# A mixture-of-experts trunk: the expert batches' gathers and adding scatters go from 96 rows to 128, with an expert's slots dealt out to other rows

## The chip, the cores and the metric

The kernel runs on one core of one Trainium2 chip. The metric is device time in microseconds (us), the median of several executions of the program. Engines are named as in the profile: PE does matmuls (PEld loads their weights), DVE and ACT do elementwise work, POOL issues indirect transfers and small set-up, SP issues plain transfers. All transfers run on the core's sixteen DMA engines.

## The reference, cut to what matters

One layer: a gated-linear-attention mixer, then a mixture of experts over 2048 tokens of 1024 numbers. Each token picks one of 8 groups and, in it, 2 of 8 experts; there are 64 experts.

```
xs = x_pad[slot_tok].reshape(n_blocks, MOE_BLOCK, dm)      # gather each expert's tokens
hid = jax.nn.silu(xb @ w1[e]) * (xb @ w3[e])               # per expert, FF = 256
return hid @ w2[e]
ys = ys * slot_gate[:, None].astype(ys.dtype)
out = jnp.zeros((n_tok + 1, dm), ys.dtype).at[slot_tok].add(ys)[:n_tok]
```

2048 tokens with 2 experts each over 64 experts make 64 tokens for an expert on average.

## The kernel before

The program has three stages in a row. `phase_gla` is the mixer. `phase_out` does the output projection, the router and the placing of tokens. `phase_moe` runs the 64 experts one after the other, and `phase_tail` normalizes and stores. All products are done in three parts (`mm3`, lines 72 to 74): each operand is split into a rounded part and a remainder.

**Slots.** Every expert has 96 early slots (`CAP`). Slot `c` of expert `e` stands in a table in memory as a pair, token number and gate weight. `first` gives an expert the slot number at which its tokens begin: 0, 4, 8 or 12, by its group. The router fills the table with small indirect scatters (`put`, line 1000). The last three token blocks don't go through the table: `part` compares each token's slot number with the tile `slot` (line 1016), `merge` turns that into a matmul that drops token and weight into the right row, and `merged` adds what the table held (tile `early`, read by six transfers at line 1080). The result is `tok` and `gate`, 96 rows by 64 experts. An empty slot holds a token number past the end, so that an indirect transfer passes over it.

Which row holds which slot is set by `slot` and by the six transfers, in the same way: row 6a+b holds slot 16b+a. Of six rows that follow each other, four hold slots below 64.

**An expert.** SP loads its weights as three tiles of 128 rows by 2048 numbers (1 MB each, line 1146). ACT and DVE split each (lines 1151 and 1154). `gather` (line 1185) fetches the expert's token rows, 4 KB each, from `s_h` in memory into 96 rows of the tile `xb`; there are three such tiles. `xtrans` turns them, `up` and `down_mm` multiply, `down` scales by the gate into the tile `y` (line 1236), and `scatter` (line 1239) adds the rows of `y` onto the rows of `s_X` in memory, as a transfer that accumulates. Gathers and scatters are issued by POOL, in program order; the loads are issued by SP as far ahead as tiles are free.

Of the kernel before, what the change touches and what calls it, by code (L numbers as in the profile page):

```python
# [11 lines left out]
F32 = mybir.dt.float32  # L12
F32R = mybir.dt.float32r
BF16 = mybir.dt.bfloat16
I32 = mybir.dt.int32
U32 = mybir.dt.uint32
AF = mybir.ActivationFunctionType
OP = mybir.AluOpType
# [3 lines left out]
S = 2048  # L22
D = 1024
# [12 lines left out]
E = 64  # L36
FF = 256
GR = 8
# [7 lines left out]
XBS = 3  # L46
YS = 3
MERGE = 3
CAP = 96
ROWS = CAP // 16  # L50
MORE = 128
SLOTS = CAP + MORE * ((S + 12 - CAP + MORE - 1) // MORE)
NSENT = 4 * S
ORDER = [i % GR * (E // GR) + i // GR for i in range(E)]
# [4 lines left out]
def split(nc, hi, lo, src, scale=None, eng=None):  # L59

    eng = eng or nc.vector
    if scale is None:
        nc.scalar.activation(hi, src, AF.Copy)  # L63
        eng.tensor_tensor(lo, src, hi.bitcast(F32), op=OP.subtract)  # L64
    else:
        nc.scalar.activation(hi, src, AF.Copy, scale=scale)
        eng.scalar_tensor_tensor(lo, src, scale, hi.bitcast(F32), op0=OP.mult, op1=OP.subtract)
# [774 lines left out]
def phase_out(tc, c, a, s, slots, ep, ex, one):  # L842

    nc = tc.nc
    with ExitStack() as ctx:
# [9 lines left out]
        iota = one.tile([128, 128], F32, name="iota")  # L855
        nc.gpsimd.iota(iota, pattern=[[1, 128]], base=0, channel_multiplier=0, allow_small_or_imprecise_dtypes=True)

        slot = one.tile([128, CAP], F32, name="slot")
        nc.gpsimd.iota(slot.rearrange("p (a b) -> p a b", b=ROWS), pattern=[[1, 16], [16, ROWS]], base=0, channel_multiplier=0,
                       allow_small_or_imprecise_dtypes=True)  # L860
        diff = one.tile([128, 128], F32, name="rdiff")
        nc.gpsimd.iota(diff, pattern=[[1, 128]], base=0, channel_multiplier=-1, allow_small_or_imprecise_dtypes=True)
        before = one.tile([128, 128], BF16, name="before")
# [4 lines left out]
        nc.gpsimd.memset(seen, 0.0)  # L868

        first = one.tile([1, E], F32, name="first")  # L870
        nc.gpsimd.iota(first.rearrange("p (a b c) -> p a b c", a=GR // 4, b=4), pattern=[[0, GR // 4], [4, 4], [0, E // GR]], base=0,
                       channel_multiplier=0, allow_small_or_imprecise_dtypes=True)
        nc.gpsimd.tensor_copy(seen[0:1, :], first)
        ent = one.tile([128, NT, 2, 2], I32, name="ent")
# [6 lines left out]
        def out_proj(t, k0, k1):  # L881
            if k0 == 0:
                PM[t] = [ps.tile([128, 512], F32, name=f"pm{i}", bufs=2) for i in range(2)]
            ep.mm(PM[t], t, k0, k1)

        def add(t):
            if t in PM:
                ep.add(PM[t], t)
# [120 lines left out]
        def part(t, pos):  # L1009

            oh = R[t][1]
            both = slots.tile(F32)
            rhs = both[:, 0:4 * E].rearrange("p (i w e) -> p i w e", i=2, w=2)
            at = both[:, 4 * E:4 * E + 2 * CAP].rearrange("p (i c) -> p i c", i=2)
            for i in range(2):
                nc.vector.tensor_scalar(at[:, i, :], slot, pos[:, i:i + 1], None, op0=OP.is_equal)
                for w, v in enumerate((gone[:, t - NT + MERGE:t - NT + MERGE + 1], ent[:, t, i, 1:2].bitcast(F32))):
                    nc.scalar.activation(rhs[:, i, w, :], oh[:, i, :], AF.Copy, scale=v)
            MG[t] = both, at, rhs

        def merge(p, ts):

            for t in ts:
                both, at, rhs = MG[t]
                for i in range(2):
                    nc.tensor.matmul(p[0:CAP], at[:, i, :], rhs[:, i].rearrange("p w e -> p (w e)"),
                                     start=(t == NT - MERGE and i == 0), stop=(t == NT - 1 and i == 1))
                slots.free(both)

        def merged(p, early):  # L1030
            nc.vector.tensor_tensor(s["tok"], p[0:CAP, 0:E], early[:, :, 0], op=OP.add)
            nc.vector.tensor_tensor(s["gate"], p[0:CAP, E:], early[:, :, 1].bitcast(F32), op=OP.add)

        s["tok"] = one.tile([CAP, E], I32, name="tok")
        s["gate"] = one.tile([CAP, E], F32, name="gate")
        gone = one.tile([128, MERGE], F32, name="gone")
        nc.gpsimd.iota(gone, pattern=[[128, MERGE]], base=S - 128 * MERGE - NSENT, channel_multiplier=1, allow_small_or_imprecise_dtypes=True)
        for t in (2, 3):
            ep.load_o(t)
            ep.load_x(t)  # L1040
        L = NT - 1
        early = one.tile([CAP, E, 2], I32, name="early")
        nc.vector.tensor_tensor(wr, wr, gcol[:, :, None].to_broadcast([128, NK, GR + E]), op=OP.mult)
        for t in range(2):
            finish(t)
# [27 lines left out]
        out_proj(L, 4, 6)  # L1073
        pos = rank(L - 2)
        part(L - 2, pos)
        logits(L - 1)
        choose(L - 1)
        out_proj(L, 6, NK)
        for b in range(ROWS):
            nc.sync.dma_start(early[b:CAP:ROWS], s["table"].rearrange("(p e) w -> p e w", e=E)[16 * b:16 * (b + 1)])  # L1080
        add(L)
        weigh(L - 1)
        address(L - 2, pos)
# [4 lines left out]
        nc.vector.tensor_tensor(hs, ep.x1[L], gff, op=OP.mult)  # L1088
        slots.free(gff, X[L][0])
        part(L - 1, pos)  # L1090
        logits(L)
        nc.scalar.activation(hs, hs, AF.Copy, scale=X[L][1])
# [6 lines left out]
        weigh(L)  # L1099
        pos = rank(L)  # L1100
        merge(last, range(NT - MERGE, L))
        part(L, pos)
        merge(last, (L,))
        merged(last, early)
        address(L, pos)
        pc = ps.tile([128, 2 * E], F32, name="pl")[:, 0:E]
# [58 lines left out]
def phase_moe(tc, c, a, s, ex, plan, rest):  # L1165
    nc = tc.nc
    with ExitStack() as ctx:
# [3 lines left out]
        xp = ctx.enter_context(tc.tile_pool(name="m_x", bufs=1, side="left", reuse_waits="tile"))  # L1171
        ex.add(left, WIDE[1])
        ident = c["ident"]
        tok = s["tok"]
        xbs = [xp.tile([128, D], F32, name=f"xb{i}") for i in range(XBS)]
        spacer = wk.tile([1, 2], F32, name="spacer2", bufs=1)
        scat = []
        XT, HID, UP, HT, PD, Y = {}, {}, {}, {}, {}, {}

        def gather(e):  # L1180
            if e >= E:
                return
            if e < XBS:
                nc.gpsimd.memset(xbs[e][0:CAP, :], 0.0)
            nc.gpsimd.indirect_dma_start(
                out=xbs[e % XBS][0:CAP, :], out_offset=None, in_=s["h"],
                in_offset=bass.IndirectOffsetOnAxis(ap=tok[:, ORDER[e]:ORDER[e] + 1], axis=0),
                bounds_check=S - 1, oob_is_err=False)

        def xtrans(e):  # L1190
            if e >= E:
                return
            p = ps.tile([128, NK, 128], F32, name="ptr")
            x = xbs[e % XBS]
            for k in range(NK):
                nc.tensor.transpose(p[:, k, 0:CAP], x[0:CAP, k * 128:(k + 1) * 128], ident[0:CAP, 0:CAP])
            hi, lo = (xp.tile([128, NK, CAP], F32R, name=n, bufs=2) for n in ("xhi", "xlo"))
            split(nc, hi, lo, p[:, :, 0:CAP])
            XT[e] = hi, lo
# [32 lines left out]
                        (whi[:, ws], wlo[:, ws]), k == 0, k == 1)  # L1232

        def down(e):
            Y[e] = xp.tile([128, D], F32, name="y", bufs=YS)
            nc.scalar.activation(Y[e][0:CAP, :], PD[e][0:CAP, :], AF.Copy, scale=s["gate"][:, ORDER[e]:ORDER[e] + 1])

        def scatter(e):
            st = nc.gpsimd.indirect_dma_start(  # L1239
                out=s["X"], out_offset=bass.IndirectOffsetOnAxis(ap=tok[:, ORDER[e]:ORDER[e] + 1], axis=0),  # L1240
                in_=Y[e][0:CAP, :], in_offset=None, bounds_check=S - 1, oob_is_err=False, compute_op=OP.add)
            for i, o in enumerate(scat):
                if i % GR != e % GR:
                    tc.declare_no_dep(st.ins, o.ins, reason="experts of different groups share no token")
            scat.append(st)
# [8 lines left out]
        for e in range(2):  # L1254
            gather(e)
        ex.split(0, 0, after_gathers)
        for _ in range(WARM):
            nc.tensor.matmul(warm[:, 0:128], ident, ident, start=True, stop=True)
        ex.split(0, 1)
        gather(2)  # L1260
        rest()
        xtrans(0)
        gather(XBS)
        for e in range(E + 1):
            live = e < E
# [23 lines left out]
            if e == 2:  # L1289
                s["plan"] = plan_more(tc, s, plan)  # L1290
        down(E - 1)
        scatter(E - 1)


# [143 lines left out]
def trunk(ctx, tc, a):  # L1438
# [18 lines left out]
    with ExitStack() as main:  # L1457
        big = main.enter_context(tc.tile_pool(name="bigs", bufs=NBIG, side="left"))
        slots = Slots()
        slots.add(big, NBIG)  # L1460
        ep = OutProj(tc, a, s, slots)
        phase_gla(tc, c, a, s, big, ep)
        plan = ctx.enter_context(tc.tile_pool(name="plan", bufs=1, side="right", reuse_waits="tile"))
        one = ctx.enter_context(tc.tile_pool(name="r_one", bufs=1, side="right", reuse_waits="tile"))
        right = ctx.enter_context(tc.tile_pool(name="wide_r", bufs=WIDE[0], side="right", reuse_waits="tile"))
        ex = Experts(tc, a)
        ex.add(right, WIDE[0])
        rest = phase_out(tc, c, a, s, slots, ep, ex, one)
    phase_moe(tc, c, a, s, ex, plan, rest)
    with ExitStack() as main:  # L1470
        big = main.enter_context(tc.tile_pool(name="tails", bufs=NTAIL, side="left", reuse_waits="tile"))
# [47 lines left out]
```

## Time and profile before

| | |
|---|---|
| time, median of 3 runs | 1634.5 us (1633.52 to 1638.4) |
| the profiled execution's own time | 1636.37 us |
| its span, first to last instruction | 1634.6 us |
| PE busy | 1524.8 us (93%) |
| DVE, ACT, POOL busy | 1099.5, 955.0, 338.6 us |
| moved by DMA | 415.22 MB, mean 254 GB/s |

Busy time is time in which an engine has an instruction in work; a matmul's end is modelled, so that a busy PE can still be waiting a little. The granted clock of PE is 0.975 of full speed over the run. The experts run from about 960 us to 1585 us. A view of the transfers gives, for a stretch, each queue's packets, the megabytes, and the time that its packets took as a share of sixteen engines; q1 is the queue of SP's loads and stores, q0 that of POOL's indirect transfers.

### The profile page before, as it was taken

To read this page: it belongs to the slowest core of one execution; us is meant where nothing else is said; L and a number is where in the kernel's file an instruction comes from. 1 tells how busy PE (TensorE), PEld (TensorE's weight loads), DVE (VectorE), ACT (ScalarE), POOL (GpSimd) and SP (SyncE) were. 2 spreads that over 40 slices of the span, in tenths; PEclk is the share of its full clock that TensorE was granted. 3 is DMA by queue.
4 is the path that set the end of the run, shared out by engine and by line. 5 is a ranking of instruction groups with operands and counts; after the bars stand their busy time and mean duration, and the time that the engine had idled before them with its cause. 6 is when DMAs were issued, how large, how long until landed. Compare 5 with 4: busy or idle time off the path is not lost.

```text
span 1634.6 us, 21425 instructions
## 1 busy us (share of the span) xinstructions
PE 1524.8 (93%) x7619; PEld 1194.5 (73%) x7619; DVE 1099.5 (67%) x2087; ACT 955.0 (58%) x1498; POOL 338.6 (21%) x248
## 2 busy tenths in 40 slices
PE   9999999999999999989999879999999999999970
PEld 7877888888888888868888757777766666666640
DVE  6566765566556655553655659989888888888855
ACT  6665544454445544432222358888788777777764
POOL 3211000000000000220211144443343333334320
PEclk9999999999999999989999989999999999999995
DMA  8545834443344434255677388999999999999969
GB/s 306 214 156 214 325 129 156 155 179 131 129 155 164 146 130 155 104 176 192 213 270 269 139 280 308 362 365 361 362 375 368 372 368 365 365 367 371 368 203 396
DMA packets 109117, 415.22 MB, mean 254 GB/s; under 512 B 19489, under 2 KB 35970, under 8 KB 84434
## 3 DMA queue, kind: packets, MB, share of 16 engines
q1 hardware_dynamic: 90242, 379.72, 62.0%
q0 software_dynamic: 15648, 33.83, 8.7%
q8 instruction: 60, 0.98, 0.2%
q10 hardware_dynamic: 3120, 0.30, 0.2%
q14 instruction: 47, 0.39, 0.1%
HBM read 345.53 MB, written 85.02 MB: 263 GB/s over the span
## 4 chain that ended last, share of the span: by engine, by line
PE 60%; DMA 29%; DVE 6%; ACT 2%; issue 1%; SPq 0%; POOL 0%; DVEq 0%; POOLq 0%; ACTq 0%
DMA wide<-w_moe 26%; PE pm L829 9%; PE pvr L72 7%; PE pvr L73 7%; PE pvr L74 7%; PE pu L73 2%; PE pu L74 2%; PE pu L72 2%; PE pk L72 2%; PE pq L72 2%; PE pq L73 2%; PE pq L74 2%; PE pk L73 2%; PE pk L74 2%; PE pl L923 2%
## 5 line engine op out<-in xcount | busy, mean ns | idle before, releaser
L1154 DVE TENSOR_TENSOR wide<-wide 128x2048 fp32r<-128x2048 f32 x192 | 438.2, 2290 | 90.6 <-ACT wide L1151 83.8
L1151 ACT ACTIVATE wide<-wide 128x2048 fp32r<-128x2048 f32 x192 | 366.0, 1914 | 87.3 <-DMA wide<-w_moe 79.2
L1239 POOL DMA_INDIRECT s_X<-y,tok x64 | 162.4, 2538 | 357.3 <-ACT ht L63 251.0
L73 PE MATMUL pu<-wide,xhi 128*96 128x512 f32 x512 | 205.5, 401 | 26.2 <-DVE wide L1154 26.2
L72 PE MATMUL pu<-wide,xhi 128*96 128x512 f32 x512 | 206.9, 404 | 0.9 <-ACT xhi L63 0.9
L74 PE MATMUL pu<-wide,xlo 128*96 128x512 f32 x512 | 203.4, 397 | 0.0
L72 PE MATMUL pvr<-big 128*128 128x512 f32 x504 | 201.3, 399 | 0.0
L73 PE MATMUL pvr<-big 128*128 128x512 f32 x504 | 197.1, 391 | 0.0
L74 PE MATMUL pvr<-big 128*128 128x512 f32 x504 | 196.8, 391 | 0.0
L829 PE MATMUL pm<-big 128*128 128x512 f32 x672 | 162.8, 398 | 5.8 <-DVE big L906 5.8
L829 PEld LDWEIGHTS pm<-big 128*128 128x128 f32 x672 | 125.6, 191 | 31.6 <-DVE big L906 6.2
L64 POOL TENSOR_TENSOR big<-big 128x1024 fp32r<-128x1024 f32 x16 | 39.3, 2468 | 519.3 <-ACT big L63 458.2
L73 PEld LDWEIGHTS pu<-wide,xhi 128*96 128x96 f32 x512 | 83.6, 163 | 71.8 <-DVE wide L1154 42.0
L72 PEld LDWEIGHTS pvr<-big 128*128 128x128 f32 x504 | 94.6, 188 | 20.5
L74 PEld LDWEIGHTS pvr<-big 128*128 128x128 f32 x504 | 94.6, 188 | 20.4
L74 PEld LDWEIGHTS pu<-wide,xlo 128*96 128x96 f32 x512 | 83.4, 163 | 34.0 <-issue 0.8
L73 PEld LDWEIGHTS pvr<-big 128*128 128x128 f32 x504 | 94.7, 188 | 18.0
L72 PEld LDWEIGHTS pu<-wide,xhi 128*96 128x96 f32 x512 | 83.3, 163 | 32.9 <-ACT xhi L63 1.2
L63 ACT ACTIVATE sp<-st 128x256 fp32r<-128x256 f32 x64 | 26.7, 416 | 137.9 <-DVE st L452 125.8
L73 PE MATMUL pd<-wide,ht 128*96 128x512 f32 x256 | 100.9, 394 | 2.2 <-DVE wide L1154 2.2
L72 PE MATMUL pd<-wide,ht 128*96 128x512 f32 x256 | 100.5, 393 | 1.2 <-ACT ht L63 1.2
L74 PE MATMUL pd<-wide,ht 128*96 128x512 f32 x256 | 100.8, 394 | 0.0
(294 smaller groups left out, 2859.5 us busy)
## 6 DMA issues: line engine op xcount, KB each, us to landing
wide<-w_moe SPq DMA_DIRECT2D x192, 1024.0 KB
big<-s_hT SPq DMA_DIRECT2D x96, 512.0 KB
s_hT<-big SPq DMA_DIRECT2D x32, 512.0 KB
s_oT<-big SPq DMA_DIRECT2D x32, 512.0 KB
big<-s_oT SPq DMA_DIRECT2D x32, 512.0 KB
big<-x SPq DMA_DIRECT2D x20, 512.0 KB
big<-w_vr SPq DMA_DIRECT2D x16, 512.0 KB
s_X<-big SPq DMA_DIRECT2D x16, 512.0 KB
```

The source lines that it names most:

```text
L63: nc.scalar.activation(hi, src, AF.Copy)
L64: eng.tensor_tensor(lo, src, hi.bitcast(F32), op=OP.subtract)
L72: nc.tensor.matmul(out, x[0], w[0], start=start, stop=False)
L73: nc.tensor.matmul(out, x[0], w[1], start=False, stop=False)
L74: nc.tensor.matmul(out, x[1], w[0], start=False, stop=stop)
L829: self.nc.tensor.matmul(pm[i], xo[:, sl], w[:, i * 512:(i + 1) * 512], start=(k == 0 and w is whi and xo is hi), stop=(k == NK - 1 and xo ...
L923: nc.tensor.matmul(pl, HT[t][:, k * 128:(k + 1) * 128], wr[:, k, :], start=(k == 0), stop=(k == NK - 1))
L1151: self.nc.scalar.activation(hi, r, AF.Copy)
L1154: self.nc.vector.tensor_tensor(lo, r, hi.bitcast(F32), op=OP.subtract)
L1239: st = nc.gpsimd.indirect_dma_start(out=s["X"], out_offset=bass.IndirectOffsetOnAxis(ap=tok[:, ORDER[e]:ORDER[e] + 1], axis=0), in_=Y[e][0 ...
```

## The change

The gathers and scatters take all 128 rows of `xb`, `tok` and `y`. Slots are dealt out by a table, `DEAL`: its entry (row, at) puts slots at to at+7 into the eight rows row, row+4, ..., row+28. Slots 0 to 63 so come to rows 0 to 31 and 64 to 95, slots 64 to 95 to rows 32 to 63, and rows 96 to 127 stay empty: `slot` holds -1 there, `early` a token number past the end. The products still use rows 0 to 95. An expert's first slot is now its group's number, 0 to 7. The table `early` is read by twelve transfers of eight rows, not six of sixteen. The three `y` tiles are allocated once, and their rows 96 to 127 are set to zero.

```
-ROWS = CAP // 16
+DEAL = [(w, (0, 16, 32, 56)[w]) for w in range(4)] + [(64 + w, (8, 24, 40, 48)[w]) for w in range(4)]
+DEAL += [(32 + w, 64 + 8 * w) for w in range(4)]
...
-        slot = one.tile([128, CAP], F32, name="slot")
-        nc.gpsimd.iota(slot.rearrange("p (a b) -> p a b", b=ROWS), pattern=[[1, 16], [16, ROWS]], base=0, channel_multiplier=0,
-                       allow_small_or_imprecise_dtypes=True)
+        slot = one.tile([128, 128], F32, name="slot")
+        nc.gpsimd.memset(slot[:, CAP:], -1.0)
+        for row, at in DEAL:
+            nc.gpsimd.iota(slot[:, row:row + 32:4], pattern=[[1, 8]], base=at, channel_multiplier=0, allow_small_or_imprecise_dtypes=True)
...
-        nc.gpsimd.iota(first.rearrange("p (a b c) -> p a b c", a=GR // 4, b=4), pattern=[[0, GR // 4], [4, 4], [0, E // GR]], base=0,
+        nc.gpsimd.iota(first.rearrange("p (a b) -> p a b", a=GR), pattern=[[1, GR], [0, E // GR]], base=0,
...
-                nc.tensor.matmul(p[0:CAP], at[:, i, :], rhs[:, i].rearrange("p w e -> p (w e)"),
+                nc.tensor.matmul(p, at[:, i, :], rhs[:, i].rearrange("p w e -> p (w e)"),
...
-        s["tok"] = one.tile([CAP, E], I32, name="tok")
-        s["gate"] = one.tile([CAP, E], F32, name="gate")
+        s["tok"] = one.tile([128, E], I32, name="tok")
+        s["gate"] = one.tile([128, E], F32, name="gate")
...
-        early = one.tile([CAP, E, 2], I32, name="early")
+        early = one.tile([128, E, 2], I32, name="early")
+        nc.gpsimd.memset(early[CAP:, :, 0], NSENT)
+        nc.gpsimd.memset(early[CAP:, :, 1], 0)
...
-        for b in range(ROWS):
-            nc.sync.dma_start(early[b:CAP:ROWS], s["table"].rearrange("(p e) w -> p e w", e=E)[16 * b:16 * (b + 1)])
+        for row, at in DEAL:
+            nc.sync.dma_start(early[row:row + 32:4], s["table"].rearrange("(p e) w -> p e w", e=E)[at:at + 8])
...
+        ys = [xp.tile([128, D], F32, name=f"y{i}") for i in range(YS)]
...
-                out=xbs[e % XBS][0:CAP, :], out_offset=None, in_=s["h"],
+                out=xbs[e % XBS], out_offset=None, in_=s["h"],
...
-            Y[e] = xp.tile([128, D], F32, name="y", bufs=YS)
-            nc.scalar.activation(Y[e][0:CAP, :], PD[e][0:CAP, :], AF.Copy, scale=s["gate"][:, ORDER[e]:ORDER[e] + 1])
+            Y[e] = ys[e % YS]
+            nc.scalar.activation(Y[e][0:CAP, :], PD[e][0:CAP, :], AF.Copy, scale=s["gate"][0:CAP, ORDER[e]:ORDER[e] + 1])
...
-                in_=Y[e][0:CAP, :], in_offset=None, bounds_check=S - 1, oob_is_err=False, compute_op=OP.add)
+                in_=Y[e], in_offset=None, bounds_check=S - 1, oob_is_err=False, compute_op=OP.add)
...
         rest()
+        for y in ys:
+            nc.gpsimd.memset(y[CAP:, :], 0.0)
```

In the program's order the change shows on two engines. On POOL, where the router's tables are set up (`slot`, `rdiff`, `ent`, `gone` are set-up tiles, `s_table` is the table), there stood before:

```order
L856 IOTA iota 128x128
L859 IOTA slot 128x96
L862 IOTA rdiff 128x128
L864 TENSOR_SCALAR before<-rdiff 128x128
L866 MEMSET onesb 128x128
L868 MEMSET seen 128x64
L871 IOTA first 1x64
L873 CAST seen<-first 1x64
L875 IOTA ent 128x32
L1037 IOTA gone 128x3
L999 MEMSET spacer 1x1
L1000 DMA s_table<-ent,addr 137216x2
```

and now:

```order
L862 MEMSET slot 128x32
L864 IOTA slot 128x8 x12
L866 IOTA rdiff 128x128
L868 TENSOR_SCALAR before<-rdiff 128x128
L870 MEMSET onesb 128x128
L872 MEMSET seen 128x64
L875 IOTA first 1x64
L877 CAST seen<-first 1x64
L879 IOTA ent 128x32
L1041 IOTA gone 128x3
L1047 MEMSET early 32x64
L1048 MEMSET early 32x64
```

One set-up instruction became thirteen, and two more stand ahead of the router's first scatter. Further on in POOL's order, where the last scatters into the table (`rest`) are followed by the gathers of experts 3 to 5 and the first adding scatter, there stood:

```order
L999 MEMSET spacer 1x1
L1000 DMA s_table<-ent,addr_9275 137216x2
L1185 DMA xb_9296<-s_h,tok 96x1024
L1185 DMA xb_9297<-s_h,tok 96x1024
L1185 DMA xb_9298<-s_h,tok 96x1024
L1239 DMA s_X<-y,tok 2048x1024
```

and now:

```order
L1004 DMA s_table<-ent,addr_9295 137216x2
L1270 MEMSET y_9319 32x1024
L1270 MEMSET y_9320 32x1024
L1270 MEMSET y_9321 32x1024
L1192 DMA xb_9316<-s_h,tok 128x1024
L1192 DMA xb_9317<-s_h,tok 128x1024
L1192 DMA xb_9318<-s_h,tok 128x1024
L1246 DMA s_X<-y_9319,tok 2048x1024
```

Three memsets come ahead of the gather of expert 3, and each gather writes 128 rows. On SP, at the end of the router, before the experts' loads:

```order
L907 DMA s_h<-big 128x1024
L1080 DMA early<-s_table 16x128 x6
L1095 DMA s_h<-big 128x1024
L897 DMA s_X<-big 128x1024
L1146 DMA wide<-w_moe 128x2048 x13
```

and now:

```order
L911 DMA s_h<-big 128x1024
L1086 DMA early<-s_table 8x128 x12
L1101 DMA s_h<-big 128x1024
L901 DMA s_X<-big 128x1024
L1152 DMA wide<-w_moe 128x2048 x13
```

Six more transfers stand ahead of the last store of `s_h`. PE, DVE and ACT keep their orders; only the shapes of the merge at the end of the router grow from 96 to 128.

## Rows read from the trace of the kernel before

**Rows 1.** Windows in the experts' stage: busy us (instructions) by engine, clock, DMA share, GB/s.

```profile
1050.00:1150.00 100.00, 100.00 (x504) 72.31 (x503) 90.02 (x66) 87.19 (x77) 43.85 (x22) 1.00 1.02 363
1150.00:1550.00 400.00, 374.80 (x1841) 261.50 (x1840) 330.68 (x240) 315.17 (x279) 149.76 (x79) 1.00 1.02 368
```

**Rows 2.** Chain that ended last, two stretches: start us, us, what.

```profile
978.79 0.66 PE ptr L1196 x8
987.94 0.66 PE ptr L1196 x8
...
1043.52 0.66 PE ptr L1196 x8
...
1049.95 25.51 DMA wide<-w_moe
...
1300.79 27.35 DMA wide<-w_moe
```

**Rows 3.** What SP's queue waited for, 1050 to 1550 us: total, times, longest.

```profile
SPq L1146 <- DMA wide<-w_moe: 412.5, 142, 4.8
SPq L1146 <- DVE wide L1154: 9.8, 7, 3.9
```

**Rows 4.** Instructions on tile `y`, 1050 to 1550 us: ACT, then POOL.

```profile
1050.00:1550.00 500.00, 55.87 (x51) 125.96 (x51) 1.00 1.02 367
```

**Rows 5.** DMA queues, 1150 to 1550 us: packets, MB, share of 16 engines.

```profile
q1 hardware_dynamic: 17289, 125.90, 80.7%
q0 software_dynamic: 8960, 20.94, 21.4%
```

**Rows 6.** DMA, 1205.6 to 1209.2 us, between a gather and a scatter.

```profile
DMA packets 251, 1.53 MB, mean 426 GB/s; under 512 B 65, under 2 KB 65, under 8 KB 65
...
q1 hardware_dynamic: 207, 1.52, 101.6%
```

**Rows 7.** DMA, 1200.1 to 1202.6 us, while a scatter runs.

```profile
q0 software_dynamic: 74, 0.27, 53.4%
q1 hardware_dynamic: 68, 0.52, 51.0%
```

**Rows 8.** DMA, 1203.9 to 1205.2 us, while a gather runs.

```profile
DMA packets 72, 0.44 MB, mean 340 GB/s; under 512 B 2, under 2 KB 2, under 8 KB 34
...
q1 hardware_dynamic: 40, 0.31, 79.0%
q0 software_dynamic: 32, 0.13, 32.5%
```

**Rows 9.** DMA, 1264.4 to 1266.6 us, while another gather runs.

```profile
DMA packets 145, 0.68 MB, mean 311 GB/s; under 512 B 42, under 2 KB 42, under 8 KB 81
...
q1 hardware_dynamic: 74, 0.52, 77.2%
```

**Rows 10.** POOL in order of time: start us, us, what, idle before.

```profile
710.93 0.44 POOL L859 IOTA slot<- 128x96 f32 x1
...
713.14 0.13 POOL L1037 IOTA gone<- 128x3 f32 x1
...
760.26 1.13 POOL L1000 DMA_INDIRECT s_table<-ent,addr  x1 [46.92 <-DVE big L839]
...
943.13 0.97 POOL L1184 MEMSET xb<- 96x1024 f32 x1
...
957.53 0.96 POOL L1000 DMA_INDIRECT s_table<-ent,addr  x1 [0.21 <-issue]
958.79 0.98 POOL L1185 DMA_INDIRECT xb<-s_h,tok  x1 [0.31 <-DMA xb<-s_h,tok]
```

**Rows 11.** SP in order of time, the end of the router.

```profile
923.88 3.79 SPq L1080 DMA_DIRECT2D early<-s_table  x6
935.70 0.34 SPq L1095 DMA_DIRECT2D s_h<-big  x1
```

**Rows 12.** Chain that ended last, the experts' first gather and last scatter.

```profile
942.12 9.71 DMA xb<-s_h,tok
...
1580.33 1.65 POOL s_X L1239
```

More of the change, by code (lines that the diff above doesn't have):

```diff
@@ L1013, in part @@
             rhs = both[:, 0:4 * E].rearrange("p (i w e) -> p i w e", i=2, w=2)
-            at = both[:, 4 * E:4 * E + 2 * CAP].rearrange("p (i c) -> p i c", i=2)
+            at = both[:, 4 * E:4 * E + 2 * 128].rearrange("p (i c) -> p i c", i=2)
             for i in range(2):
@@ L1030, in merged @@
         def merged(p, early):
-            nc.vector.tensor_tensor(s["tok"], p[0:CAP, 0:E], early[:, :, 0], op=OP.add)
-            nc.vector.tensor_tensor(s["gate"], p[0:CAP, E:], early[:, :, 1].bitcast(F32), op=OP.add)
-        s["tok"] = one.tile([CAP, E], I32, name="tok")
-        s["gate"] = one.tile([CAP, E], F32, name="gate")
+            nc.vector.tensor_tensor(s["tok"], p[:, 0:E], early[:, :, 0], op=OP.add)
+            nc.vector.tensor_tensor(s["gate"], p[:, E:], early[:, :, 1].bitcast(F32), op=OP.add)
+        s["tok"] = one.tile([128, E], I32, name="tok")
+        s["gate"] = one.tile([128, E], F32, name="gate")
         gone = one.tile([128, MERGE], F32, name="gone")
```

## The prediction

> **What bounds the kernel now.** The change touches the experts' stage, so I look only at where that stage's time goes. The windows come first: from 1050 to 1550 us the sixteen DMA engines have a share of 1.02, that is, no idle time (it passes 1 because neighbouring packets overlap a little), while PE falls from fully busy in the first 100 us to 374.80 of the next 400 [rows 1]. Then the chain of waits: up to 1050 us it runs through PE, whose steps can be read off the transposes of `xb`, one set an expert: 9.15 us from 978.79 to 987.94, and 64.73 us for the seven steps to 1043.52, 9.25 each. From 1049.95 on it runs through the loads, in pieces such as 25.51 and 27.35 us [rows 2]. SP's own waits agree: 412.5 us of that half millisecond until an earlier load had landed, 9.8 for a tile that DVE still read [rows 3]. So PE works off a store of loaded weights at first; later each expert takes what the DMA engines need for it. That is the number to work on.
>
> Its size: an expert's loads are 3.146 MB, so the 125.90 MB that q1 moved in 400 us are 40.0 experts, 10.0 us each [rows 5]. Over 1050 to 1550 us ACT wrote 51 tiles `y` [rows 4]; that is PE's count, which still has its quick first steps in it.
>
> **Where a DMA engine's 10.0 us go.** An expert gives each engine 24 load packets of 8 KB (3.146 MB over 16 engines), and on average 4 gather packets and 4 scatter packets of 4 KB (64 tokens over 16). q1's 80.7% of 400 us over 40 experts is 8.07 us, or 336 ns a packet; q0's 21.4% is 2.14 us [rows 5]. Three short stretches price them.
> - Loads alone: 1.52 MB are 186 packets, 101.6% of 16 engines over 3.6 us is 58.5 us, so 315 ns a packet, at 426 GB/s [rows 6].
> - Beside a scatter: 0.52 MB are 63 packets in 20.4 us, 323 ns; the scatter's 66 take 324 ns each [rows 7]. The two alternate on every engine, and the loads hardly suffer.
> - Beside a gather: 40 packets in 16.4 us, 411 ns, and 32 gather packets in 6.8 us, 211 ns, at 340 GB/s [rows 8]. A second gather: 0.52 MB are 63 packets, 77.2% of 16 engines over 2.2 us is 27.2 us, 430 ns, at 311 GB/s [rows 9].
>
> So a gather slows itself and the loads beside it by a third, a scatter doesn't. A gather writes rows of SBUF, as the loads do; a scatter reads them. The loads write 128 rows and don't slow each other; the gather writes 96. What a gather costs above its bytes is therefore the disputed sum: 24 x (336 - 315) = 0.50 us on the loads, and on the gathers themselves, with 4 x 324 = 1.30 us of the 2.14 for scatters, 0.84 left for four gathers, 0.21 each against half a load packet, 0.157: another 0.21. Together 0.71 of the 10.21 busy us, 7%.
>
> **The change part by part.**
> *Gathers and scatters over 128 rows.* The tokens moved are the same, and the empty rows are passed over now as before (20.94 MB of q0 in 40 experts are 128 packets each, no more than the tokens need [rows 5]). The price of the clash is bounded by 0 (nothing about the gather's packets changes but the rows) and by the whole 0.71 (the gather then behaves like the other transfer that writes 128 rows, the load [rows 6]). I take 0.6: the nearest row is the load's, a little off because overlapped packets are counted twice in a share of 1.02 [rows 1]. That makes 10.0 into 9.4 us.
> The trace shows no rows of a tile, so it can't say which engine writes which. [...]
>
> *How many experts it is worth.* The loads set the pace from 1050 to about 1550 us, 50 experts of 10.0 us: 50 x 0.6 = 30 us. PE has a floor under it: 51 steps [rows 4] of 9.2 us (between 9.15 and 9.25 [rows 2]) are 469 of the 500 us, so no more than 31 can be won. Both limits lie close together, and two streams of nearly one pace wait for each other now and then; I take 27.
>
> [...]
>
> *POOL.* A scatter into the table handles 128 indices in 0.96 us, a gather 96 in 0.98 [rows 10], so 32 more cost between 0 and a third (0.33 us). POOL is busy 149.76 of 400 us [rows 1]: hidden, but for the first gather, on the chain with 9.71 us, and the last scatter, with 1.65 [rows 12]: 0 to 0.3 and 0 to 0.55 us. The set-up's one instruction of 0.44 us becomes thirteen at 0.13 to 0.44, and two memsets: 1.5 to 6 us, ahead of a scatter that sat 46.92 us idle [rows 10]. The three memsets of `y` (at 0.97, like that of `xb`) move the gather of expert 3 from 958.79 by 2.9 us [rows 10]; its rows are wanted at the fourth set of transposes, after 987.94 [rows 2]. Without that cover it would be 2.9 us once.
>
> *SP.* Six reads of `early` took 3.79 us of issue, 0.63 each; twelve take 7.6 and end at 931.5, ahead of the store at 935.70, which waits for its data [rows 11]. Half of them could run into a wait for an earlier one to land, and there are four microseconds for it. Without that cover: at most 3.8 us once, since the first loads queue behind.
>
> *DVE and PE.* Compares and merge over 128 columns in place of 96: the only one on the chain is the last pair, under 0.2 us.
>
> Sum: -27, +0.5 for first gather, last scatter and compares: about -27. The profiled execution took 1636.37 us, 1.8 around its span and 1.9 above the median of the runs; it becomes 1609.4, and the median **1607.5**.
>
> **The rivals.**
> *Half of it.* The new rows take away only part of the clash. For: the gather's own packets still come between the loads'. Half the price is 0.3 an expert, 15 us: 1620.
>
> *Nothing.* The slowing is that of two reads of memory on one engine, whatever rows they land in. Against: a scatter reads memory as well, and beside it the loads stay at 323 ns [rows 7]. [...] Then 1635, 0 to 1 us more. [...]
>
> *Slower.* An engine is given eight rows that follow each other, as it must have been given six of the 96: while a scatter runs, q0 and q1 hold 53.4 and 51.0% of the sixteen engines [rows 7], so all sixteen share it, which fits four live rows in each six. With eights, rows 0 to 31 and 64 to 95 belong to eight engines, and these have eight live rows each where they had four. Their expert costs 24 x 315 + 8 x 157 + 8 x 324 = 11.4 us if nothing clashes, 24 x 336 + 8 x 210 + 8 x 324 = 12.3 if it does; less the overlap, 11.2 to 12.0 against 10.0. It decides from the fifth live row on, since each further one costs 0.48 and only 0.6 is to be won. Over 50 experts 60 to 100 us: about 1715. For it: sixes before. Against: the loads of 128 rows don't clash, so they are not cut in a way that makes them.
>
> **How the numbers follow.** A measurement of this kernel can tell about 0.3%, 5 us, from no change. The forecast has 0.64, half of it 0.17, nothing 0.08, slower 0.11. The first two are faster by more than 5 us: 0.81; same 0.08; slower 0.11. The forecast's own range is 1600 (all 31 us of PE's floor, and a few more from the first gather) to 1614 (two thirds of the price). To hold 8 in 10 the range takes in the half case: 1598 to 1632. The slow rival, far off, is left out.
>
> **What would show it.** Right: load packets beside a gather near 315 ns and gather packets near 160; q1's share for 40 experts near 76%, q0's near 20%; the stage's GB/s up from 368 to 385 or more; the chain on PE well past 1050 us, with steps of 9.2; SP waiting for tiles rather than landings. Half right: beside a gather 350 to 380 ns. Wrong if gathers still slow the loads to 411, or if a scatter of 64 rows takes twice as long with half the engines on it. POOL's gather above 1.3 us, or the store of `s_h` later than 936 us, would show costs that I put at nothing.

## The result, and the profile after

The changed kernel takes 1598.6 us (median of 4 runs, 1597.1 to 1600.1) against 1634.0 for the kernel before: a ratio of 0.978, 95% interval 0.9767 to 0.9792. That is 35.4 us less, where 27 were forecast (1607.5; the range was 1598 to 1632). The profiled execution took 1600.11 us, 36.3 less than that of before. The measured time lies 0.6 us inside the end of the range, and outside the forecast's own range of 1600 to 1614.

The profile page of the changed kernel: its span, the chain by engine, and what memory read and wrote.

```profile
span 1598.3 us, 21450 instructions
...
HBM read 353.92 MB, written 93.41 MB: 280 GB/s over the span
...
PE 88%; DVE 5%; DMA 3%; ACT 2%; issue 1%; SPq 0%; POOL 0%; DVEq 0%; POOLq 0%; ACTq 0%
```

In the kernel before, the chain by engine was:

```profile
PE 60%; DMA 29%; DVE 6%; ACT 2%; issue 1%; SPq 0%; POOL 0%; DVEq 0%; POOLq 0%; ACTq 0%
```

DMA's share of the chain fell from 29% to 3%. The windows of the experts' stage, to set beside [rows 1] (PE, PEld, DVE, ACT, POOL busy, clock, DMA share, GB/s):

```profile
1050.00:1150.00 100.00, 100.00 (x505) 72.34 (x504) 90.09 (x67) 87.17 (x77) 45.71 (x22) 1.00 1.02 394
1150.00:1450.00 300.00, 300.00 (x1512) 217.06 (x1511) 270.35 (x197) 261.73 (x231) 139.56 (x66) 1.00 1.02 392
```

PE stays fully busy, and the transfers move 392 GB/s where they moved 368; the DMA engines are as full as before (a share of 1.02 in both). The chain of waits (start us, us, what), to set beside [rows 2, 12]:

```profile
940.60 9.38 DMA xb<-s_h,tok
...
1042.04 0.66 PE ptr L1203 x8
1051.17 0.66 PE ptr L1203 x8
1060.32 0.66 PE ptr L1203 x8
...
1508.57 0.66 PE ptr L1203 x8
...
1526.88 0.66 PE ptr L1203 x8
...
1543.03 1.77 POOL s_X L1246
...
1547.68 5.71 DMA s_X<-y,tok
```

and the last transposes of the kernel before:

```profile
1564.20 0.66 PE ptr L1196 x8
```

The chain no longer leaves PE: 50 steps from 1051.17 to 1508.57 are 9.15 us each. From the first gather to the last scatter that the chain shows on POOL it takes 602.4 us (940.60 to 1543.03), where it took 638.2 [rows 12]: 35.8 of the 36.3 us. The rest is 1.5 us less ahead of the first gather and 1.0 more behind that scatter. All of the 35.8 us lie in the last 53 steps: 484.84 us now (1042.04 to 1526.88), 520.68 before (1043.52 [rows 2] to 1564.20).

What ACT's splits of the loads (line 1157, in the kernel before line 1151) waited for tells the same. In the kernel before, idle us and times:

```profile
  DMA wide<-w_moe: 79.2, 101
```

and in the changed kernel, where the loads are no longer among the causes:

```profile
  PE pd L76: 6.4, 18
  DVE hid L1222: 0.3, 1
```

SP's own waits from 1050 to 1550 us, to set beside [rows 3]:

```profile
SPq L1152 <- DMA wide<-w_moe: 210.1, 87, 4.0
SPq L1152 <- PE pu L77: 40.1, 18, 4.0
SPq L1152 <- PE pd L77: 37.0, 15, 4.6
SPq L1152 <- DVE wide L1160: 36.1, 16, 4.3
```

Half of SP's waiting for landings is gone; it now waits as well for tiles that PE and DVE still read. The transfers of the changed kernel, in three stretches: 1050 to 1530 us, then 1209.6 to 1212.4 with loads alone, then 1207.5 to 1208.9 beside a gather (to set beside [rows 5, 6, 8]):

```profile
q1 hardware_dynamic: 22100, 160.95, 80.1%
q0 software_dynamic: 14908, 26.88, 21.8%
...
DMA packets 181, 1.18 MB, mean 421 GB/s; under 512 B 37, under 2 KB 37, under 8 KB 37
...
q1 hardware_dynamic: 160, 1.17, 99.6%
...
DMA packets 127, 0.60 MB, mean 430 GB/s; under 512 B 37, under 2 KB 37, under 8 KB 70
...
q1 hardware_dynamic: 65, 0.47, 79.0%
q0 software_dynamic: 62, 0.14, 24.6%
```

and the long stretch in the kernel before:

```profile
q1 hardware_dynamic: 20640, 150.29, 80.4%
q0 software_dynamic: 10948, 25.49, 21.6%
```

Beside the gather, 0.47 MB are 57 packets of 8 KB in 17.7 us of engine time (79.0% of 16 engines over 1.4 us): 310 ns each, where it was 411 and 430 [rows 8, 9] (the first is 432 by the 38 packets of 8 KB that its 0.31 MB make). Loads alone: 143 packets in 44.6 us, 312 ns. The gather's 0.14 MB are 34 packets in 5.5 us, 162 ns where it was 211. The packets beside a gather are as quick as those alone. Over the long stretch 160.95 MB are 51.2 experts, 9.38 us each, where 150.29 MB were 47.8 experts, 10.05 us each.

POOL (start us, us, what, idle before), to set beside [rows 10]:

```profile
709.14 0.13 POOL L862 MEMSET slot<- 128x32 f32 x1
709.21 1.05 POOL L864 IOTA slot<- 128x8 f32 x12
...
712.26 0.15 POOL L1048 MEMSET early<- 32x64 int32 x1
...
757.97 1.10 POOL L1004 DMA_INDIRECT s_table<-ent,addr  x1 [45.42 <-DVE seen L998]
...
957.16 2.73 POOL L1270 MEMSET y<- 32x1024 f32 x3
960.05 1.04 POOL L1192 DMA_INDIRECT xb<-s_h,tok  x1 [0.16 <-issue]
```

and SP at the end of the router, to set beside [rows 11]:

```profile
922.22 8.21 SPq L1086 DMA_DIRECT2D early<-s_table  x12
934.04 0.34 SPq L1101 DMA_DIRECT2D s_h<-big  x1
```

From `slot` to its end the set-up takes 3.3 us where it took 2.3 [rows 10], ahead of 45 us of idle time. The memsets hold the gather of expert 3 up by 2.7 us, and PE's steps don't show it. The twelve reads end at 930.4, 3.6 us ahead of the store.

### The profile page after: what moved, and what is told of

Its sections match the earlier page's. It is cut to its first block, busy times and chain, and to the rows that moved or that the text cites. A ratio compares the mean times of both kernels' runs of the same rounds, so it can differ in the third digit from the quotient of the medians.

```text
span 1598.3 us, 21450 instructions
## 1 busy us (share of the span) xinstructions
PE 1514.1 (95%) x7619; PEld 1197.2 (75%) x7619; DVE 1096.7 (69%) x2087; ACT 957.0 (60%) x1498; POOL 365.9 (23%) x265
## 2 busy tenths in 40 slices
DMA packets 113213, 415.24 MB, mean 260 GB/s; under 512 B 23585, under 2 KB 40066, under 8 KB 88530
## 4 chain that ended last, share of the span: by engine, by line
PE 88%; DVE 5%; DMA 3%; ACT 2%; issue 1%; SPq 0%; POOL 0%; DVEq 0%; POOLq 0%; ACTq 0%
PE pm L832 9%; PE pu L77 7%; PE pu L76 7%; PE pu L75 7%; PE pvr L75 7%; PE pvr L76 7%; PE pvr L77 7%; PE pd L76 4%; PE pd L75 4%; PE pd L77 4%; PE ptr L1203 3%; PE pk L75 2%; PE pq L75 2%; PE pq L76 2%; PE pq L77 2%; PE pk L76 2%
## 5 line engine op out<-in xcount | busy, mean ns | idle before, releaser
L1246 POOL DMA_INDIRECT s_X<-y,tok x64 | 187.5, 2929 | 297.8 <-ACT y L1243 283.3
```

Source lines behind the costliest of these rows:

```text
L1246: st = nc.gpsimd.indirect_dma_start(out=s["X"], out_offset=bass.IndirectOffsetOnAxis(ap=tok[:, ORDER[e]:ORDER[e] + 1], axis=0), in_=Y[e], ...
```

## The experiments

The theory, a supposition of the author's, since no view names the engine of a packet: an engine that gathers six of 96 rows writes rows that, in a load, another engine writes, and the two slow each other (load packets above 410 ns beside a gather, 315 alone [rows 6, 8, 9]); with 128 rows an engine gathers into the rows that it loads. The rivals: the gain is from the new dealing of slots, from the scatter, or from the new start numbers; or PE isn't the floor. Each ratio is to runs of the kernel before that were taken along with it (medians 1633.6 to 1634.4 us). The pace in the table is 300 us over the experts that q1's bytes between 1150 and 1450 us make (3.146 MB each), by the same view for each kernel.

| kernel | time, us | ratio to before (95%) | us of loads an expert |
|---|---|---|---|
| before | 1634 | | 10.00 |
| changed | 1598.6 | 0.978 (0.9767 to 0.9792) | 9.41 |
| g128_old | 1612.4 | 0.9874 (0.9857 to 0.9891) | 9.56 |
| s128_old | 1663.6 | 1.0179 (1.0162 to 1.0196) | 10.40 |
| s96_new | 1635.7 | 1.001 (1.000 to 1.002) | 10.05 |
| rows64 | 1639.4 | 1.0038 (1.0025 to 1.0051) | 10.02 |
| deal_0_63 | 1697.7 | 1.0389 (1.0368 to 1.0409) | 11.07 |
| before_3g | 1599.0 | 0.9793 (0.9771 to 0.9814) | 9.10 |
| after_3g | 1597.6 | 0.9776 (0.9757 to 0.9796) | 9.10 |
| first_old | 1601.7 | 0.9806 (0.9785 to 0.9827) | 9.39 |

**The gather alone (g128_old).** In the kernel before:

```
-                out=xbs[e % XBS][0:CAP, :], out_offset=None, in_=s["h"],
+                out=xbs[e % XBS], out_offset=None, in_=s["h"],
...
-        s["tok"] = one.tile([CAP, E], I32, name="tok")
+        s["tok"] = one.tile([128, E], I32, name="tok")
+        nc.gpsimd.memset(s["tok"][CAP:, :], NSENT)
```

> The kernel before with one thing changed: the gather takes 128 rows (rows 96 to 127 hold an empty token number); the slots stay dealt out as before, and the scatter keeps its 96 rows. Clash theory (the gain is all from the 128-row gather no longer slowing the loads beside it): load packets beside a gather about 310 ns, gather packets 159 ns as in the changed kernel; the old dealing leaves eight engines 5.3 gathered rows an expert and eight 2.7, so 24 x 312 + 5.3 x 159 + 4 x 327 = 9.65 us an expert, hardly above PE's 9.16: 1604 us (1598 to 1612). Rival (the gain is from the new dealing of slots or from the scatter): 1630 us or more, loads beside a gather still about 410 ns.

1612.4 us, 0.4 above the expected range. Its transfers beside a gather, 1196.6 to 1198.6 us:

```profile
DMA packets 181, 0.86 MB, mean 428 GB/s; under 512 B 58, under 2 KB 58, under 8 KB 95
...
q1 hardware_dynamic: 93, 0.70, 83.2%
```

0.70 MB are 85 packets in 26.6 us: 312 ns. So the 128 rows of the gather take the clash away by themselves, with the old dealing, and bring 22 of the 35 us. What is left is put down to the uneven split of the old dealing: 9.56 us an expert, where the sum had 9.65 without the overlap. The sum's 5.3 and 2.7 rows an engine are the author's estimate; no view shows them.

**The scatter alone (s128_old).** In the kernel before, `y` allocated and cleared as in the changed kernel, and:

```
-                in_=Y[e][0:CAP, :], in_offset=None, bounds_check=S - 1, oob_is_err=False, compute_op=OP.add)
+                in_=Y[e], in_offset=None, bounds_check=S - 1, oob_is_err=False, compute_op=OP.add)
```

> The kernel before with one thing changed: the adding scatter takes 128 rows, from y tiles allocated once; slots and gather as before. Clash theory: the gather still slows the loads (about 410 ns beside it), and with the old dealing eight engines have 5.3 rows to scatter and eight 2.7: 24 x 336 + 4 x 194 + 5.3 x 327 = 10.6 us an expert against 10.15 before by the same sum: 1652 us (1640 to 1662). Rival (the scatter's 128 rows bring part of the gain): below 1625 us.

1663.6 us, 1.6 above the range: the scatter's 128 rows bring nothing, and with the old dealing they cost 29 us.

**The scatter back on 96 rows (s96_new).** In the changed kernel:

```
-                in_=Y[e], in_offset=None, bounds_check=S - 1, oob_is_err=False, compute_op=OP.add)
+                in_=Y[e][0:CAP, :], in_offset=None, bounds_check=S - 1, oob_is_err=False, compute_op=OP.add)
```

> The changed kernel with the scatter back on 96 rows; the slots stay dealt out the new way, the gather keeps its 128 rows. Clash theory, with an engine taking six rows that follow each other out of 96: gathers and loads stay quick (159 and 312 ns), but ten engines have six rows to scatter and the others next to none: 24 x 312 + 4 x 159 + 6 x 327 = 10.1 us an expert: 1628 us (1618 to 1642), and a scatter of 64 rows takes about 3.9 us where it took 2.6. Rival (which rows an engine scatters doesn't matter): 1599 us.

1635.7 us, inside the expected range: all of the gain is lost. The gather is as quick as in the changed kernel. Beside one, 1197.1 to 1199.0 us:

```profile
q1 hardware_dynamic: 94, 0.66, 82.8%
q0 software_dynamic: 59, 0.14, 18.0%
```

0.66 MB are 81 packets in 25.2 us, 312 ns; the gather's 34 take 161 ns. So of these two scatters the new dealing fits the one of 128 rows (1598.6 us against 1635.7), and the scatter had to go along because a slot has one row for both. The expectation's ten engines with six rows are the author's estimate; no view shows them.

**Rows 0 to 63 (rows64).** In the changed kernel:

```
+DEAL = [(w, 16 * w) for w in range(4)] + [(32 + w, 16 * w + 8) for w in range(4)]
+DEAL += [(64 + w, 64 + 8 * w) for w in range(4)]
...
-                out=xbs[e % XBS], out_offset=None, in_=s["h"],
+                out=xbs[e % XBS][0:64, :], out_offset=None, in_=s["h"],
...
-                in_=Y[e], in_offset=None, bounds_check=S - 1, oob_is_err=False, compute_op=OP.add)
+                in_=Y[e][0:64, :], in_offset=None, bounds_check=S - 1, oob_is_err=False, compute_op=OP.add)
```

> The changed kernel with gather and scatter on rows 0 to 63 alone, each one transfer of 64 rows, and the first 64 slots dealt out evenly over these (four rows that follow each other hold slots c, c+16, c+32, c+48); the slots above 63, about one in twenty, are left out of the computation. Each engine has four rows of gather and scatter, as even as can be. Clash theory, with rows 32 to 63 written by engines other than those that write them in a load: loads beside a gather 400 ns or more, gather packets 200 or more, 1625 us (1612 to 1650). Rival (an even split is all that counts): loads 312 ns, 1590 to 1600 us, a little quicker than the changed kernel for its fewer rows.

1639.4 us, with fewer rows to move and, by the expectation's count, an even split. Beside a gather, 1202.2 to 1204.1 us:

```profile
DMA packets 111, 0.58 MB, mean 304 GB/s; under 512 B 19, under 2 KB 19, under 8 KB 62
...
q1 hardware_dynamic: 58, 0.40, 74.0%
q0 software_dynamic: 53, 0.18, 31.5%
```

0.40 MB are 49 packets in 22.5 us, 460 ns; 44 gather packets in 9.6 us, 218 ns. The clash is back, and worse than before. What is read from memory is the same as in the changed kernel but for the rows left out. These are 9%, not one in twenty: DMA moved 412.31 MB where it moved 415.24, and half of the 2.93 MB less are 358 of 4096 gathered rows. So the slowing goes with the rows that are written, 64 or 96 of them (load packets of 460 ns beside 64, above 410 beside 96 [rows 8, 9], 310 beside 128), and not with the reads.

**The dealing (deal_0_63).** In the changed kernel:

```
+DEAL = [(w, (0, 16, 32, 56)[w]) for w in range(4)] + [(32 + w, (8, 24, 40, 48)[w]) for w in range(4)]
+DEAL += [(64 + w, 64 + 8 * w) for w in range(4)]
```

> The changed kernel with two blocks of rows exchanged in the table: slots 0 to 63 on rows 0 to 63, slots above 63 on rows 64 to 95; gather and scatter keep 128 rows. If an engine takes four neighbouring rows and the four 32 further on, as the theory has it, eight engines now hold eight live rows each: 24 x 312 + 8 x 159 + 8 x 327 = 11.4 us an expert, so 1710 us (1690 to 1730), and a scatter of 64 rows takes twice as long. Rival (128 rows are enough, wherever the slots stand; or an engine takes every sixteenth row): 1599 us.

1697.7 us, inside the expected range and far from the rival's 1599. While a scatter runs, 1252.8 to 1256.8 us:

```profile
q1 hardware_dynamic: 137, 0.99, 67.5%
q0 software_dynamic: 136, 0.23, 29.9%
```

q0 holds 29.9% of sixteen engines where a scatter of the kernel before held 53.4% [rows 7]: little over half, as if half of the engines had all the rows. With slots 0 to 63 on rows 0 to 31 and 64 to 95 the time is 1598.6 us, with the same slots on rows 0 to 63 it is 1697.7. The reading is that rows 0 to 31 and 32 to 63 belong to the same eight engines; the finer split that the expectation supposes, which rows go to one engine, no run shows.

The run also answers a rival that the forecast did not name: that the changed gather is quick because its 64 empty rows space out its packets. While a gather runs, 1235.9 to 1237.3 us:

```profile
DMA packets 84, 0.46 MB, mean 331 GB/s; under 512 B 17, under 2 KB 17, under 8 KB 38
...
q1 hardware_dynamic: 55, 0.38, 63.8%
q0 software_dynamic: 29, 0.09, 15.2%
```

0.38 MB are 46 packets in 14.3 us, 311 ns, and 21 gather packets in 3.4 us, 162 ns. By that reading the eight engines now have hardly an empty row between their full ones, and in this stretch neither the loads nor the gather is slowed. A longer one, 1235.9 to 1238.9 us:

```profile
q1 hardware_dynamic: 106, 0.76, 75.1%
q0 software_dynamic: 58, 0.18, 14.8%
```

The 1.6 us that it adds hold, by difference, about 46 load packets in 21.8 us, 470 ns, and 22 gather packets in 3.7 us, 168 ns. The gather is as quick there, the loads are not; over 1150 to 1450 us they average 352 ns (85.28 MB at 76.3% of sixteen engines), where the changed kernel's average 313 (100.30 MB at 79.9%). What slows them in this run isn't shown. So the run speaks against the rival by the gather's own packets, and by the loads only in the shorter stretch. What stays open is also what makes a gather of 64 or 96 rows slow: no view names the engine of a packet, so that two engines meet at the same rows is the reading that fits the runs, and it isn't seen directly.

**Without gathers (before_3g and after_3g).** In both kernels:

```
-            if e >= E:
+            if e >= XBS:
                 return
```

> The kernel before with only the first three gathers issued; the other 61 experts compute on what stands in the three tiles, so gathered tokens are left out of the result. Clash theory (the gather is all that held the loads back): loads 312 ns, 24 x 312 + 4 x 327 = 8.8 us an expert, below PE's 9.16, so PE sets the pace: 1599 us (1595 to 1603), as the changed kernel. Rival (the loads are slow for another reason as well): above 1610 us.

> The changed kernel with only the first three gathers issued; the other 61 experts compute on what stands in the three tiles, so gathered tokens are left out of the result. If PE is the floor of the changed kernel, gathers cost it nothing more: 1598 us (1595 to 1600). Rival (the transfers still set the pace in part): 1585 to 1593 us.

1599.0 and 1597.6 us. Without its gathers the kernel before runs as quickly as the changed one with them, and the changed one gains 1.0 us without them, which can't be told from nothing. What SP waited for in before_3g, 1050 to 1550 us:

```profile
SPq L1146 <- PE pu L74: 95.1, 35, 4.0
SPq L1146 <- PE pd L74: 81.1, 25, 5.0
SPq L1146 <- DVE wide L1154: 79.5, 31, 4.3
```

No landing of a load is among its waits, and PE is busy 300.00 of the 300 us from 1150 to 1450: PE sets the pace.

**The start numbers (first_old).** In the changed kernel, the old line of `first`:

> The changed kernel with the first slot numbers of before (0, 4, 8, 12 by group, not 0 to 7). More slots then lie above 63, on eight of the engines. By the reference's routing an expert has 2.5 slots more there on average, a fifth to a third of a row for each of eight engines: 0.1 to 0.15 us an expert, and PE's pace hides part: 1599 to 1603 us. Rival (the new start numbers carry part of the gain): above 1605 us.

1601.7 us: 3 us more, inside the expected range; a small part, and at the edge of what can be told.

## Why the prediction was right

**What bounds the stage** held: the loads' pace set it before [rows 2, 3], and ACT's 79.2 us of waiting for loads are gone.

**The clash** held in its place. The forecast put it on the rows that the gather writes, from one contrast: loads slow beside a gather, not beside a scatter [rows 7, 8]. The gather alone on 128 rows and the 64-row gather show it from both sides (load packets of 312 and 460 ns beside them); that engines meet at the same rows is, as said, inferred. Of the disputed 0.71 us, 0.67 are measured between the same stretches by bytes (10.05 us an expert against 9.38, 1050 to 1530 us). The forecast had 0.6. In busy time of an engine, q1's part fell from 8.08 to 7.51 us an expert and q0's from 2.17 to 2.05: 0.57 and 0.12, where the forecast's terms were 0.50 and 0.21.

**The sizes** were too small, each a little, which makes 35 of 27. Three terms. The price, 0.67 and not 0.6, over about 50 experts: 3 us; by the table's stretch it is 0.59, and this term next to nothing. The stretch: I counted from 1050 us, but gathers slowed the loads from 977 on, while PE ran off the store. From 977 to 1050 us q1 now moves 21.10 MB and moved 19.52, half an expert, 5 us of loads more in store. And the tenth that I took off for two streams of one pace waiting for each other: the store that PE works off, fuller and drained by 0.2 us an expert (9.38 against 9.15) where it was by 0.9, lasted to the end, so they never met. Together these would make 38 us, and by bytes it comes to about as much: from 977 to 1530 us q1 moved 12.24 MB more than before, 3.9 experts or 37 to 39 us of loads. PE's floor let 36 through. The floor was right in kind: 9.15 us a step where I took 9.2 (the 9.25 of [rows 2] had one step of 9.81 in it, from 987.94 to 997.75). It binds the last 53 steps, which took 9.82 us each before. So both limits were put too low, the loads' at 30 us and PE's at 31.

**The split of the rows.** No change was put down for it. How many rows an engine has, before or after, no run shows; the runs show what other dealings cost, which the forecast had only in its slow rival: 14 us (g128_old), 29 (s128_old), 37 (s96_new) and 99 (deal_0_63), each against the kernel that it was made from, but g128_old against the changed one, so that its 14 hold the 3 us of the start numbers too. That an uneven split is the cause is the author's estimate, by the 2.7 to eight rows an engine in the expectations' sums; no run shows these terms, and in their place stand the measured paces, 9.56 us an expert (9.65 by the sum), 10.40 (10.6), 10.05 (10.1) and 11.07 (11.4). The rival of eight rows that follow each other is out: with it, deal_0_63 would be no worse than the changed kernel, and it takes 1697.7 us against 1598.6.

**The costs at nothing** held: SP ended its reads 3.6 us ahead of the store; POOL's extra work lay in idle time, and its set-up grew by 0.9 us where 1.5 to 6 were put down. The first gather's 9.71 us are 9.38, the last scatter's 1.65 are 1.77.

## What to carry to other kernels

When transfers fill all DMA engines (a share of 1.02 here), price their packets apart: alone (315 ns here), beside each of the other kinds (323 beside a scatter, above 410 beside a gather). Here a third more beside one kind and not beside another was a clash, and its cause was looked for in what the two do not have in common. Then time the split that the transfer really has, since s96_new, the same dealing with a scatter of 96 rows, lost all that the clash had cost (1635.7 us against 1598.6). And when a second engine's floor lies close under the gain (here PE's 9.15 us a step under the loads' 9.38), ask how long its store of work lasts at the new pace; if to the end, as here, the floor is the forecast.

## What the runs showed that I had not expected

The profile's line on memory counts empty rows. It reads, for the kernel before, for the gather alone on 128 rows (g128_old) and for the scatter alone (s128_old):

```profile
HBM read 345.53 MB, written 85.02 MB: 263 GB/s over the span
...
HBM read 353.92 MB, written 85.02 MB: 273 GB/s over the span
...
HBM read 345.53 MB, written 93.41 MB: 264 GB/s over the span
```

Both differences are 8.39 MB, 64 experts by 32 rows by 4 KB, rows that no packet of that size moved: the changed kernel has 23585 packets under 512 B, where the kernel before had 19489, 4096 more, one for each added row of 64 gathers and 64 scatters.

On POOL 32 more rows cost a gather 0.06 us (0.98 to 1.04). A scatter's median in the stage went from 2.37 to 3.08 us, but not for its rows: with 128 rows it is 2.49 in s128_old and 2.50 in deal_0_63, and with 96 rows 2.92 in before_3g. So the rows cost about 0.1 us, and the rest goes with the quicker pace that PE sets; why stays open. It is hidden here, at a POOL that is busy 139.56 of 300 us.

The stretch ahead of the router, which nothing changed, differs between profiles by more than the small terms of the sum: POOL's first instruction of it starts at 707.2 to 710.7 us over the ten profiles.
